# Row means over 536 MB: one single row at each end, zones of 94, 18 and 16 rows, and a last row shared with ScalarE

## The chip, the cores and the metric

The kernel runs on one core of one Trainium2 chip. The metric is device time in microseconds (us): the median of several executions. The time before is 1243.16 us, the median of three runs (1243.15 to 1243.31).

## The reference

The input is 64 x 256 x 8192 numbers in float32, and the output is the mean over the last axis:

```
def setup_inputs():
    return {
        "x": np.random.randn(64, 256, 8192).astype(np.float32),
    }

def reference(x: np.ndarray) -> np.ndarray:
    return np.mean(x, axis=2)
```

That is 16384 rows of 8192 numbers (32 KB a row), each summed and multiplied by 1/8192. 536.87 MB are read and 64 KB written.

## The kernel before, in words

The 16384 rows are spread over 128 partitions, so every partition owns 128 rows (OWN). They aren't dealt out as one block. ZONE = [95, 17, 16] (L27) cuts the rows of memory in three zones: in the first zone each partition owns 95 neighbouring rows, in the second 17, in the third 16. Inside a zone the rows of one partition lie one behind the other in memory, and the next partition begins 95, 17 or 16 rows further on: the row stride of the zone. Each zone has a store of its own at the end.

The work is a stream of pairs. A pair is two rows for each of the 128 partitions, 64 KB a partition and 8 MB in all. Three buffers (buf0 to buf2) of 64 KB a partition hold one pair each. The order of everything is written out by hand for each engine, with semaphores between them:

- SyncE (SP) issues all DMAs on one queue. It first issues the pair for buf0, which is a mixed one: the upper half is the first row of zone 1, in two pieces of 1 MB and 3 MB (L108, L109), and the lower half is the last row of zone 0 (L112). Two pairs for buf1 and buf2 follow (L114). Then a loop of 15 rounds (ROUNDS, L118) waits until a buffer is free and loads the next pair of zone 0 into it (L121), and 15 loads written out one by one do the rest (L127). The last two rows come in five pieces (L133, the bounds in cuts, L43); the fifth goes to a small tensor of its own, fin. SP then waits for GpSimd, stores zones 0 and 1 (L136), waits for the very last sum and stores zone 2 (L140).
- VectorE (DVE) reduces one pair with one tensor_reduce (L168, in a loop of 20 rounds of three; L178 for two of the last three). Pair 62, the last whole one, and the last two rows are summed by the helper halves (L149, L151): it adds the first half of a piece to its second half, element by element, and accumulates the sum over the columns in the same instruction. A piece of n columns so costs an instruction of n/2 columns.
- ScalarE (ACT) sums a share of four of the five last pieces (mine, L44) with an activation that copies and accumulates (L207). Its partial sums and those of VectorE are written behind the fifth piece in fin, so that the last halves (L199) sums the fifth piece and all partial sums at once and scales them.
- GpSimd (POOL) multiplies the sums by 1/8192 (L97) in four operations, after all rows but the last are summed.

A buffer's way round is: SP loads it (in_sems), VectorE reduces it (free_sems), SP loads it again. The change touches the sizes (L27 to L46), the order of loads in SP, the tail of VectorE and ScalarE, and GpSimd's operations.

Of the kernel before, what the change touches and what calls it, by code (L numbers as in the profile page):

```python
# [6 lines left out]
ADD = mybir.AluOpType.add  # L7
X = mybir.AxisListType.X
COPY = mybir.ActivationFunctionType.Copy


def bass_global_avg_pool_1d_kernel(
# [4 lines left out]
    P = 128  # L17
    ALIGN = 4096
    B, C, L = x.shape
    rows = B * C  # L20
    inv = 1.0 / float(L)

    OWN = rows // P
    ZONE = [95, 17, 16]  # L27
    FROM = [0, ZONE[0], ZONE[0] + ZONE[1]]
    EARLY, LATE = FROM[2], ZONE[2]
    NB = OWN // 2 - 1  # L30
    NBUF = 3
    PAIRS0 = ZONE[0] // 2
    ROUNDS = PAIRS0 // NBUF
    assert rows % P == 0 and sum(ZONE) == OWN and NB % NBUF == 0
    assert ZONE[0] % 2 == 1 and ZONE[1] % 2 == 1
    assert (PAIRS0 + 1) % NBUF == 0 and NB - PAIRS0 - 1 > NBUF
    LOADS0 = (NB - PAIRS0 - 1) // NBUF
    first_row = lambda g: 2 * g - 2 if g <= PAIRS0 else 2 * g
    FIRST = L // 4


    U = L // 256
    cuts = [0, L + 29 * U, L + 169 * U, L + 217 * U, L + 240 * U, 2 * L]  # L43
    mine = [29 * U, 50 * U, 17 * U, 8 * U]  # L44
    LAST = cuts[5] - cuts[4]
    NPART = 8  # L46

    flat = x.rearrange("b c l -> (b c) l")
    out_flat = out.rearrange("b c -> (b c)")
    zone = [  # L50
        flat[P * f : P * (f + n), :].rearrange("(p r) l -> p (r l)", p=P)
        for f, n in zip(FROM, ZONE)
    ]
# [2 lines left out]
        for f, n in zip(FROM, ZONE)  # L56
    ]

    with ExitStack() as ctx:
        sb = lambda n, s: ctx.enter_context(nc.sbuf_tensor(n, s, F32))  # L60
        sem = lambda n: ctx.enter_context(nc.semaphore(n))
        res = sb("res", [P, OWN - 1])
        scaled = sb("scaled", [P, EARLY])
        ends = sb("ends", [P, LATE])
        fin = sb("fin", [P, LAST + NPART])
        sb("pad", [P, (-nc.sbuf_base % ALIGN) // 4])
        bufs = [sb(f"buf{i}", [P, 2 * L]) for i in range(NBUF)]

        in_sems = [sem(f"in_sem{i}") for i in range(NBUF)]
        free_sems = [sem(f"free_sem{i}") for i in range(NBUF)]  # L70
        first_sem = sem("first_sem")
        mixed_sem = sem("mixed_sem")
        chunk_sems = [sem(f"chunk_sem{c}") for c in range(5)]
        owned_sem = sem("owned_sem")
        part_d = sem("part_d")
        part_a = sem("part_a")
        pool_sem = sem("pool_sem")
        late_sem = sem("late_sem")
        out_sem = sem("out_sem")
        end_sem = sem("end_sem")  # L80

        tail = bufs[0]
        part = lambda n: fin[:, LAST + n : LAST + n + 1]

        eng = nc.gpsimd
        eng.memset(part(NPART - 1), 0.0).then_inc(part_d, 1)  # L88
        eng.wait_ge(free_sems[0], LOADS0 + 1)
        eng.wait_ge(owned_sem, 4)  # L90
        for dst, src in [
            (scaled[:, 0 : ZONE[0] - 1], res[:, 2 : ZONE[0] + 1]),
            (scaled[:, ZONE[0] - 1 : ZONE[0] + 1], res[:, 0:2]),
            (scaled[:, ZONE[0] + 1 : EARLY], res[:, ZONE[0] + 1 : EARLY]),
            (ends[:, 0 : LATE - 1], res[:, EARLY : OWN - 1]),
        ]:
            eng.tensor_scalar(dst, src, inv, None, op0=mybir.AluOpType.mult).then_inc(  # L97
                pool_sem, 1
            )


        eng = nc.sync
        def rows_of(n, k):
            z = 2 if n >= FROM[2] else 1 if n >= FROM[1] else 0
            return zone[z][:, (n - FROM[z]) * L : (n - FROM[z] + k) * L]

        a, z = rows_of(ZONE[0] - 1, 1), rows_of(ZONE[0], 1)
        eng.dma_start(bufs[0][:, L : L + FIRST], z[:, 0:FIRST]).then_inc(first_sem, 16)  # L108
        eng.dma_start(bufs[0][:, L + FIRST : 2 * L], z[:, FIRST:L]).then_inc(  # L109
            mixed_sem, 16  # L110
        )
        eng.dma_start(bufs[0][:, 0:L], a).then_inc(in_sems[0], 16)  # L112
        for g in range(1, NBUF):
            eng.dma_start(bufs[g][:], rows_of(first_row(g), 2)).then_inc(in_sems[g], 16)  # L114
        src = rows_of(first_row(NBUF), ROUNDS * NBUF * 2).rearrange(
            "p (i b w) -> b p i w", i=ROUNDS, b=NBUF
        )
        with eng.Fori(0, ROUNDS) as i:  # L118
            for b in range(NBUF):
                eng.wait_ge(free_sems[b], 1).then_inc(free_sems[b], -1)  # L120
                eng.dma_start(bufs[b][:], src[b][:, bass.ds(i, 1), :]).then_inc(  # L121
                    in_sems[b], 16
                )
        for g in range(PAIRS0 + 1, NB):
            b = g % NBUF
            eng.wait_ge(free_sems[b], (g - PAIRS0 - 1) // NBUF + 1)
            eng.dma_start(bufs[b][:], rows_of(first_row(g), 2)).then_inc(in_sems[b], 16)  # L127
        eng.wait_ge(free_sems[0], LOADS0 + 1)
        two = rows_of(2 * NB, 2)
        for c in range(5):  # L130
            a, z = cuts[c], cuts[c + 1]
            dst = tail[:, a:z] if c < 4 else fin[:, 0:LAST]
            eng.dma_start(dst, two[:, a:z]).then_inc(chunk_sems[c], 16)  # L133
        eng.wait_ge(pool_sem, 4)
        for z in range(2):
            eng.dma_start(  # L136
                out_zone[z], scaled[:, FROM[z] : FROM[z] + ZONE[z]]
            ).then_inc(out_sem, 16)
        eng.wait_ge(late_sem, 1)
        eng.dma_start(out_zone[2], ends[:]).then_inc(end_sem, 16)  # L140
        eng.wait_ge(out_sem, 32)
        eng.wait_ge(end_sem, 16)

        eng = nc.vector

        def halves(ap, to, done, scale=1.0):  # L149
            n = ap.shape[1] // 2  # L150
            eng.tensor_tensor_reduce(  # L151
                ap[:, 0:n],
                ap[:, 0:n],
                ap[:, n : 2 * n],
                scale=scale,
                scalar=0.0,
                op0=ADD,
                op1=ADD,
                accum_out=to,
            ).then_inc(done, 1)  # L160

        eng.wait_ge(first_sem, 16)
        eng.wait_ge(mixed_sem, 16)
        sums = res[:, 0 : 2 * (NB - NBUF)].rearrange("p (i b j) -> p i b j", b=NBUF, j=2)
        with eng.Fori(0, NB // NBUF - 1) as i:
            for b in range(NBUF):
                eng.wait_ge(in_sems[b], 16).then_inc(in_sems[b], -16)  # L167
                eng.tensor_reduce(  # L168
                    sums[:, bass.ds(i, 1), b, :],
                    bufs[b][:].rearrange("p (j l) -> p j l", j=2),  # L170
                    X,
                    ADD,
                ).then_inc(free_sems[b], 1)
        for b in range(NBUF):
            g = NB - NBUF + b
            eng.wait_ge(in_sems[b], 16)
            if b < 2:
                eng.tensor_reduce(  # L178
                    res[:, 2 * g : 2 * g + 2],
                    bufs[b][:].rearrange("p (j l) -> p j l", j=2),  # L180
                    X,
                    ADD,
                ).then_inc(free_sems[0] if b == 0 else owned_sem, 1)
            else:
                for j in range(2):
                    halves(
                        bufs[b][:, j * L : (j + 1) * L],
                        res[:, 2 * g + j : 2 * g + j + 1],
                        owned_sem,
                    )  # L190
        eng.wait_ge(chunk_sems[0], 16)
        halves(tail[:, 0:L], res[:, 2 * NB : 2 * NB + 1], owned_sem)
        for c in range(1, 4):
            eng.wait_ge(chunk_sems[c], 16)
            halves(tail[:, cuts[c] + mine[c] : cuts[c + 1]], part(3 + c), part_d)
        eng.wait_ge(chunk_sems[4], 16)
        eng.wait_ge(part_a, 4)
        eng.wait_ge(part_d, 4)
        halves(fin, ends[:, LATE - 1 : LATE], late_sem, inv)  # L199


        eng = nc.scalar
        for c in range(4):
            eng.wait_ge(chunk_sems[c], 16)
            a = cuts[c] if c else L
            ap = tail[:, a : a + mine[c]]
            eng.activation(ap, ap, COPY, accum_out=part(c)).then_inc(part_a, 1)  # L207


# [26 lines left out]
```

## Time and profile before

| what | value |
|---|---|
| median of the runs | 1243.16 us (1243.15 to 1243.31) |
| the profiled execution | 1243.06 us |
| its span, first to last instruction | 1241.7 us |
| VectorE busy | 1084.1 us, 76 instructions |
| ScalarE busy | 5.2 us |
| GpSimd busy | 2.9 us |
| moved by DMA | 536.94 MB, 432 GB/s over the span |

The profile is that of one execution, and its 1243.06 us is 1.36 us longer than its span: that is time before the first and after the last instruction. "Idle before" in a row is the time that the engine waited just ahead of the instructions in it, with what ended the wait. The chain is followed back from the last instruction. Windows give the busy time of each engine between two points of the span, with the DMA engines' busy share and their rate at the end of the line. The timeline's first column is the start in us from the start of the span, and the second is the duration. A row of a DMA issue ends with the time from issue to landing.

### The profile page before, as it was taken

What the parts mean: (1) busy time and instruction counts of PE and PEld (TensorE: products, weight loads), DVE (VectorE), ACT (ScalarE), POOL (GpSimd) and SP (SyncE); (2) the same over time, 40 slices, a digit from 0 to 9 for tenths busy, and PEclk for the clock granted to TensorE, in tenths of its full rate; (3) what the DMA queues carried; (4) which work ended last, traced back from release to release, by engine and by line L of the source; (5) the groups of instructions that cost most, each with busy time, mean ns of one, the idle gap of its engine ahead of it and who ended that gap; (6) DMA issues with size and microseconds to landing.
All of it is one profiled execution on the core that took longest, in us unless ns stands there. A gap on an engine that the chain in (4) does not pass through costs nothing. (4 is left out here: it accounts for less than half of the span.)

```text
span 1241.7 us, 549 instructions
## 1 busy us (share of the span) xinstructions
DVE 1084.1 (87%) x76; ACT 5.2 (0%) x9; POOL 2.9 (0%) x9
## 2 busy tenths in 40 slices
DVE  2898988989889898898898988989889898898987
ACT  0000000000000000000000000000000000000001
POOL 0000000000000000000000000000000000000000
DMA  9999999999999999999999999999999999999998
GB/s 405 439 439 439 439 435 410 439 439 439 439 439 433 412 439 439 439 439 439 426 418 439 439 439 439 439 422 422 439 439 439 439 439 422 422 439 439 439 439 374
DMA packets 10512, 536.94 MB, mean 432 GB/s; under 512 B 1552, under 2 KB 1552, under 8 KB 1936
## 3 DMA queue, kind: packets, MB, share of 16 engines
q1 hardware_dynamic: 10512, 536.94, 99.9%
HBM read 536.87 MB, written 0.07 MB: 432 GB/s over the span
## 5 line engine op out<-in xcount | busy, mean ns | idle before, releaser
L168 DVE TENSOR_REDUCE res<-buf 128x16384 f32 x60 | 1033.2, 17220 | 146.5 <-DVEq L167 146.5
L178 DVE TENSOR_REDUCE res<-buf 128x2 f32<-128x16384 f32 x2 | 34.4, 17220 | 4.0 <-DMA buf<-in_x_dram 4.0
L151 DVE CUSTOM_DVE_ANT_0 buf<-buf 128x4096 f32<-128x4096 f32 (+3 forms) x6 | 16.0, 2672 | 5.4 <-DMA buf<-in_x_dram 5.4
L207 ACT ACTIVATE buf<-buf 128x928 f32<-128x928 f32 (+3 forms) x4 | 3.6, 897 | 1233.7 <-DMA buf<-in_x_dram 1233.7
L97 POOL TENSOR_SCALAR scaled<-res 128x94 f32<-128x94 f32 (+2 forms) x3 | 2.4, 784 | 1235.0 <-DVE res L151 1234.8
L207 ACT ACT_TABLE_LOAD x1 | 1.3, 1283 | 0.7 <-PEq L221 0.7
L207 ACT ACTIVATION_READ_ACCUMULATOR buf<-buf 128x1 f32 x4 | 0.7, 187 | 0.0
L151 DVE CUSTOM_DVE_ANT_0 fin<-fin 128x260 f32<-128x260 f32 x1 | 0.4, 429 | 0.3 <-DMA fin<-in_x_dram 0.3
L97 POOL TENSOR_SCALAR ends<-res 128x15 f32<-128x15 f32 x1 | 0.3, 264 | 0.1
L151 DVE DVE_READ_ACCUMULATOR2_ANT res<- 128x1 f32 x3 | 0.3, 84 | 0.0
L151 DVE DVE_READ_ACCUMULATOR2_ANT fin<- 128x1 f32 x3 | 0.2, 81 | 0.0
L221 POOL MEMSET const-bfloat16-1.0<- 128x1 bf16 x1 | 0.1, 102 | 0.0
L221 POOL MEMSET const-uint8-127<- 128x1 uint8 x1 | 0.1, 102 | 0.0
L88 POOL MEMSET fin<- 128x1 f32 x1 | 0.1, 99 | 0.3 <-POOLq L221 0.3
L221 POOL MEMSET const-float32-0.0<- 128x1 f32 x1 | 0.1, 99 | 0.2 <-issue 0.2
L221 POOL MEMSET const-float32-1.0<- 128x1 f32 x1 | 0.1, 99 | 0.0
L151 DVE DVE_READ_ACCUMULATOR2_ANT ends<- 128x1 f32 x1 | 0.1, 82 | 0.0
## 6 DMA issues: line engine op xcount, KB each, us to landing
buf<-in_x_dram SPq DMA_DIRECT2D x1, 4560.0 KB, 32.2
buf<-in_x_dram SPq DMA_DIRECT2D x1, 4096.0 KB, 20.6
buf<-in_x_dram SPq DMA_DIRECT2D x1, 3072.0 KB, 11.4
buf<-in_x_dram SPq DMA_DIRECT2D x1, 2240.0 KB, 37.1
buf<-in_x_dram SPq DMA_DIRECT2D x1, 1024.0 KB, 4.6
buf<-in_x_dram SPq DMA_DIRECT2D x62, 40.3
buf<-in_x_dram SPq DMA_DIRECT2D x1, 768.0 KB, 38.5
buf<-in_x_dram SPq DMA_DIRECT2D x1, 368.0 KB, 39.0
```

The costliest lines, as they stand in the source:

```text
L88: eng.memset(part(NPART - 1), 0.0).then_inc(part_d, 1)
L97: eng.tensor_scalar(dst, src, inv, None, op0=mybir.AluOpType.mult).then_inc(pool_sem, 1)
L151: eng.tensor_tensor_reduce(ap[:, 0:n], ap[:, 0:n], ap[:, n : 2 * n], scale=scale, scalar=0.0, op0=ADD, op1=ADD, accum_out=to,).then_inc(do ...
L168: eng.tensor_reduce(sums[:, bass.ds(i, 1), b, :], bufs[b][:].rearrange("p (j l) -> p j l", j=2), X, ADD,).then_inc(free_sems[b], 1)
L178: eng.tensor_reduce(res[:, 2 * g : 2 * g + 2], bufs[b][:].rearrange("p (j l) -> p j l", j=2), X, ADD,).then_inc(free_sems[0] if b == 0 els ...
L207: eng.activation(ap, ap, COPY, accum_out=part(c)).then_inc(part_a, 1)
L221: nc = _bacc.Bacc("TRN2", target_bir_lowering=False, num_devices=1)
```

## The change

- The stream begins with one single row (the first of zone 2), in two pieces of 1 MB and 3 MB, in the lower half of buf2. VectorE sums it with halves, and a new semaphore, first_done, tells SP that buf2 may be loaded with pair 2.
- 63 pairs follow, all of rows of one zone. The zones are 94, 18 and 16 rows, so that zones 0 and 1 hold whole pairs, and zone 2 holds its first row, seven pairs and its last row. The loop in SP has 14 rounds instead of 15, and 18 loads instead of 15 are written out.
- The last pair (pair 62, in buf2) has a semaphore of its own, pair_sem. VectorE sums its first row and the first quarter of its second row; ScalarE sums the other three quarters (6144 columns) into side.
- One single row comes last, in four pieces of 4992, 1920, 768 and 512 columns, where two rows came in five pieces of 9120, 4480, 1536, 736 and 512 columns. ScalarE takes 1856, 640 and 224 columns of the first three.
- GpSimd scales rows 0 to 111 in one operation as soon as buf0 has been reduced for pair 57, and SP issues the stores of zones 0 and 1 right behind the last four loads. GpSimd later adds the two parts of the shared row (tensor_tensor), waits for that, and scales the 14 inner columns of zone 2. VectorE scales the first and the last row of zone 2 itself.

The diff, cut to its core:

```diff
-    ZONE = [95, 17, 16]
+    ZONE = [94, 18, 16]
...
-    ROUNDS = PAIRS0 // NBUF
+    ROUNDS = PAIRS0 // NBUF - 1
+    SINGLE = NBUF * (ROUNDS + 1)
...
-    cuts = [0, L + 29 * U, L + 169 * U, L + 217 * U, L + 240 * U, 2 * L]
-    mine = [29 * U, 50 * U, 17 * U, 8 * U]
+    cuts = [0, 156 * U, 216 * U, 240 * U, L]
+    mine = [58 * U, 20 * U, 7 * U]
...
+    def pair(g, k=1):
+        z = 0 if 2 * g < FROM[1] else 1 if 2 * g < FROM[2] else 2
+        a = 2 * g - FROM[z] + (z == 2)
+        return zone[z][:, a * L : (a + 2 * k) * L]
...
         eng = nc.gpsimd
-        eng.memset(part(NPART - 1), 0.0).then_inc(part_d, 1)
-        eng.wait_ge(free_sems[0], LOADS0 + 1)
-        eng.wait_ge(owned_sem, 4)
-        for dst, src in [
-            (scaled[:, 0 : ZONE[0] - 1], res[:, 2 : ZONE[0] + 1]),
-            (scaled[:, ZONE[0] - 1 : ZONE[0] + 1], res[:, 0:2]),
-            (scaled[:, ZONE[0] + 1 : EARLY], res[:, ZONE[0] + 1 : EARLY]),
-            (ends[:, 0 : LATE - 1], res[:, EARLY : OWN - 1]),
-        ]:
-            eng.tensor_scalar(dst, src, inv, None, op0=mybir.AluOpType.mult).then_inc(
-                pool_sem, 1
-            )
+        eng.wait_ge(free_sems[0], turn(NB) - 1)
+        eng.tensor_scalar(
+            scaled[:], res[:, 0:EARLY], inv, None, op0=mybir.AluOpType.mult
+        ).then_inc(pool_sem, 1)
+        eng.wait_ge(free_sems[0], turn(NB))
+        eng.wait_ge(owned_sem, 3)
+        eng.wait_ge(side_a, 1)
+        eng.tensor_tensor(
+            res[:, 2 * NB - 1 : 2 * NB], side[:, 0:1], side[:, 1:2], op=ADD
+        ).then_inc(joined_sem, 1)
+        eng.wait_ge(joined_sem, 1)
+        eng.tensor_scalar(
+            ends[:, 1 : LATE - 1], res[:, EARLY : 2 * NB], inv, None,
+            op0=mybir.AluOpType.mult,
+        ).then_inc(pool_sem, 1)
...
         eng = nc.sync
+        eng.dma_start(single[:, 0:FIRST], zone[2][:, 0:FIRST]).then_inc(first_sem, 16)
+        eng.dma_start(single[:, FIRST:L], zone[2][:, FIRST:L]).then_inc(mixed_sem, 16)
+        for g in range(NBUF):
+            if g == NBUF - 1:
+                eng.wait_ge(first_done, 1)
+            eng.dma_start(bufs[g][:], pair(g)).then_inc(in_sems[g], 16)
...
-        for g in range(PAIRS0 + 1, NB):
+        for g in range(SINGLE, NB):
             b = g % NBUF
-            eng.wait_ge(free_sems[b], (g - PAIRS0 - 1) // NBUF + 1)
-            eng.dma_start(bufs[b][:], rows_of(first_row(g), 2)).then_inc(in_sems[b], 16)
-        eng.wait_ge(free_sems[0], LOADS0 + 1)
-        two = rows_of(2 * NB, 2)
-        for c in range(5):
+            eng.wait_ge(free_sems[b], turn(g))
+            eng.dma_start(bufs[b][:], pair(g)).then_inc(
+                in_sems[b] if g < NB - 1 else pair_sem, 16
+            )
+        eng.wait_ge(free_sems[0], turn(NB))
+        row = zone[2][:, (LATE - 1) * L : LATE * L]
+        for c in range(4):
...
-        eng.wait_ge(pool_sem, 4)
+        eng.wait_ge(pool_sem, 1)
         for z in range(2):
             eng.dma_start(
                 out_zone[z], scaled[:, FROM[z] : FROM[z] + ZONE[z]]
             ).then_inc(out_sem, 16)
+        eng.wait_ge(pool_sem, 2)
         eng.wait_ge(late_sem, 1)
...
         eng = nc.vector
...
         eng.wait_ge(mixed_sem, 16)
+        halves(single, ends[:, 0:1], first_done, inv)
...
+        eng.wait_ge(pair_sem, 16)
+        halves(both[:, 0:L], res[:, 2 * NB - 2 : 2 * NB - 1], owned_sem)
+        halves(both[:, L : L + SIDE], side[:, 0:1], owned_sem)
+        for c in range(3):
             eng.wait_ge(chunk_sems[c], 16)
-            halves(tail[:, cuts[c] + mine[c] : cuts[c + 1]], part(3 + c), part_d)
-        eng.wait_ge(chunk_sems[4], 16)
-        eng.wait_ge(part_a, 4)
-        eng.wait_ge(part_d, 4)
+            halves(tail[:, cuts[c] + mine[c] : cuts[c + 1]], part(c), part_d)
+        eng.wait_ge(chunk_sems[3], 16)
+        eng.wait_ge(part_a, 3)
+        eng.wait_ge(part_d, 3)
         halves(fin, ends[:, LATE - 1 : LATE], late_sem, inv)
...
         eng = nc.scalar
+        eng.wait_ge(pair_sem, 16)
+        ap = both[:, L + SIDE : 2 * L]
+        eng.activation(ap, ap, COPY, accum_out=side[:, 1:2]).then_inc(side_a, 1)
+        for c in range(3):
             eng.wait_ge(chunk_sems[c], 16)
-            a = cuts[c] if c else L
-            ap = tail[:, a : a + mine[c]]
-            eng.activation(ap, ap, COPY, accum_out=part(c)).then_inc(part_a, 1)
+            ap = tail[:, cuts[c] : cuts[c] + mine[c]]
+            eng.activation(ap, ap, COPY, accum_out=part(3 + c)).then_inc(part_a, 1)
```

Here U is 32 columns, L is 8192, NB is 63, LATE is 16, EARLY is 112 and SIDE is 2048. turn(g) is the count that free_sems must have reached for the load of pair g.

More of the change, by code (lines that the diff above doesn't have):

```diff
@@ L32, in bass_global_avg_pool_1d_kernel @@
     PAIRS0 = ZONE[0] // 2
-    ROUNDS = PAIRS0 // NBUF
+    ROUNDS = PAIRS0 // NBUF - 1
+    SINGLE = NBUF * (ROUNDS + 1)
     assert rows % P == 0 and sum(ZONE) == OWN and NB % NBUF == 0
[L35 to L38, printed above, removed]
+    assert all(z % 2 == 0 for z in ZONE) and 2 * (NB - NBUF) >= EARLY
+    turn = lambda g: (g - SINGLE) // NBUF + 1
     FIRST = L // 4
     U = L // 256
-    cuts = [0, L + 29 * U, L + 169 * U, L + 217 * U, L + 240 * U, 2 * L]
-    mine = [29 * U, 50 * U, 17 * U, 8 * U]
-    LAST = cuts[5] - cuts[4]
-    NPART = 8
+    cuts = [0, 156 * U, 216 * U, 240 * U, L]
+    mine = [58 * U, 20 * U, 7 * U]
+    LAST = cuts[4] - cuts[3]
+    NPART = 6
+    SIDE = L // 4
     flat = x.rearrange("b c l -> (b c) l")
@@ L72, in bass_global_avg_pool_1d_kernel @@
         mixed_sem = sem("mixed_sem")
-        chunk_sems = [sem(f"chunk_sem{c}") for c in range(5)]
+        first_done = sem("first_done")
+        pair_sem = sem("pair_sem")
+        chunk_sems = [sem(f"chunk_sem{c}") for c in range(4)]
         owned_sem = sem("owned_sem")
@@ L102, in bass_global_avg_pool_1d_kernel @@
-        eng = nc.sync
[L103 to L112, printed above, removed]
@@ L113, in bass_global_avg_pool_1d_kernel @@
-        for g in range(1, NBUF):
-            eng.dma_start(bufs[g][:], rows_of(first_row(g), 2)).then_inc(in_sems[g], 16)
-        src = rows_of(first_row(NBUF), ROUNDS * NBUF * 2).rearrange(
+        eng.wait_ge(free_sems[0], turn(NB) - 1)
[8 more added lines that the diff above has]
+        ).then_inc(joined_sem, 1)
@@ L116, in bass_global_avg_pool_1d_kernel @@
+        src = pair(NBUF, ROUNDS * NBUF).rearrange(
             "p (i b w) -> b p i w", i=ROUNDS, b=NBUF
@@ L173, in bass_global_avg_pool_1d_kernel @@
                 ).then_inc(free_sems[b], 1)
-        for b in range(NBUF):
-            g = NB - NBUF + b
+        for g in range(NB - NBUF, NB - 1):
+            b = g % NBUF
             eng.wait_ge(in_sems[b], 16)
[L177 to L190, printed above, removed]
@@ L191, in bass_global_avg_pool_1d_kernel @@
-        eng.wait_ge(chunk_sems[0], 16)
-        halves(tail[:, 0:L], res[:, 2 * NB : 2 * NB + 1], owned_sem)
-        for c in range(1, 4):
+            eng.tensor_reduce(
+                res[:, 2 * g : 2 * g + 2],
+                bufs[b][:].rearrange("p (j l) -> p j l", j=2),
+                X,
+                ADD,
+            ).then_inc(free_sems[0] if b == 0 else owned_sem, 1)
+        eng.wait_ge(pair_sem, 16)
+        halves(both[:, 0:L], res[:, 2 * NB - 2 : 2 * NB - 1], owned_sem)
+        halves(both[:, L : L + SIDE], side[:, 0:1], owned_sem)
@@ L202, in bass_global_avg_pool_1d_kernel @@
         eng = nc.scalar
-        for c in range(4):
+        eng.wait_ge(pair_sem, 16)
+        ap = both[:, L + SIDE : 2 * L]
+        eng.activation(ap, ap, COPY, accum_out=side[:, 1:2]).then_inc(side_a, 1)
+        for c in range(3):
             eng.wait_ge(chunk_sems[c], 16)
-            a = cuts[c] if c else L
-            ap = tail[:, a : a + mine[c]]
-            eng.activation(ap, ap, COPY, accum_out=part(c)).then_inc(part_a, 1)
+            ap = tail[:, cuts[c] : cuts[c] + mine[c]]
+            eng.activation(ap, ap, COPY, accum_out=part(3 + c)).then_inc(part_a, 1)
```

11 lines of the change are left out of this document (8 added, 3 removed).

## The prediction

> **What bounds the kernel now.** I read the page first: busy shares and slices, then the chain that ended last, then the transfers.
>
> ```profile
> DVE 1084.1 (87%) x76; ACT 5.2 (0%) x9; POOL 2.9 (0%) x9
> ...
> DMA  9999999999999999999999999999999999999998
> GB/s 405 439 439 439 439 435 410 439 439 439 439 439 433 412 439 439 439 439 439 426 418 439 439 439 439 439 422 422 439 439 439 439 439 422 422 439 439 439 439 374
> DMA packets 10512, 536.94 MB, mean 432 GB/s; under 512 B 1552, under 2 KB 1552, under 8 KB 1936
> ...
> DMA buf<-in_x_dram 3%; DMA fin<-in_x_dram 3%; DVE res L168 1%; DVE res L178 1%; SPq L133 0%; DVE fin L151 0%; DVEq L168 0%; DVE ends L151 0%
> ```
>
> The DMA engines are full in every slice but the last, and VectorE has 13% to spare. The dips in GB/s look like five hiccups. They are counting: at 434 GB/s one of 16 engines needs 65536 B x 16 / 434 GB/s = 2.42 us for a 64 KB packet, so a slice of 31.04 us holds 13 packet ends (439 GB/s) or 12 (405). If the stream really hiccuped, reductions would start late somewhere. The windows by zone, between starts of reductions, show that they don't:
>
> ```profile
> 22.49:930.65 908.16, 809.34 (x47) 0.00 (x0) 0.00 (x0) 1.00 1.00 434
> 930.65:1104.51 173.86, 154.98 (x9) 0.00 (x0) 0.00 (x0) 1.00 1.00 434
> 1104.51:1220.27 115.76, 103.32 (x7) 0.00 (x0) 0.00 (x0) 1.00 0.99 431
> ```
>
> First window: pairs 0 to 46, zone of 95 rows, 908.16 / 47 = 19.323 us a pair. Second: about the zone of 17, 173.86 / 9 = 19.318. Third: the zone of 16, six intervals (its seventh start is its end), 19.293. The timeline explains the odd one:
>
> ```profile
> 22.49 17.22 DVE L168 TENSOR_REDUCE res<-buf 128x16384 f32 x1 [22.49 <-DVEq L167]
> ...
> 39.99 19.66 SPq L121 DMA_DIRECT2D buf<-in_x_dram  x2
> ```
>
> ```profile
> 1162.48 17.22 DVE L168 TENSOR_REDUCE res<-buf 128x16384 f32 x1 [2.07 <-DVEq L167]
> ...
> 1181.58 17.22 DVE L178 TENSOR_REDUCE res<-buf 128x2 f32<-128x16384 f32 x1 [1.89 <-DMA buf<-in_x_dram]
> ...
> 1200.96 17.22 DVE L178 TENSOR_REDUCE res<-buf 128x2 f32<-128x16384 f32 x1 [2.16 <-DMA buf<-in_x_dram]
> 1220.27 4.42 DVE L151 CUSTOM_DVE_ANT_0 buf<-buf 128x4096 f32<-128x4096 f32 x1 [2.09 <-DMA buf<-in_x_dram]
> ```
>
> The step from the loop (1162.48) to the first reduction outside it (1181.58) is 19.10 us, the next one 19.38: inside the loop a reduction starts some 0.2 us later after its data. Corrected by 0.2, the third window is (115.76 + 0.2) / 6 = 19.327. So three row strides, 95, 17 and 16 rows, run within 0.01 us of 19.323 us a pair: the rate of the stream doesn't depend on the zone. A reduction takes 17.22, so 2.1 us are spare in every pair.
>
> The start is read from issue and landing:
>
> ```profile
> 0.73 0.39 SPq L108 DMA_DIRECT2D buf<-in_x_dram  x1
> 1.17 0.43 SPq L109 DMA_DIRECT2D buf<-in_x_dram  x1
> 1.65 0.42 SPq L112 DMA_DIRECT2D buf<-in_x_dram  x1
> ```
>
> ```profile
> buf<-in_x_dram SPq DMA_DIRECT2D x1, 4096.0 KB, 20.6
> buf<-in_x_dram SPq DMA_DIRECT2D x1, 3072.0 KB, 11.4
> ...
> out_dram<-scaled SPq DMA_DIRECT2D x1, 47.5 KB, 1.6
> out_dram<-scaled SPq DMA_DIRECT2D x1, 8.5 KB, 1.6
> out_dram<-ends SPq DMA_DIRECT2D x1, 8.0 KB, 1.4
> ```
>
> The first row is complete at 1.17 + 11.4 = 12.57, the first pair at 1.65 + 20.6 = 22.25. And the end, from the chain and the timeline:
>
> ```profile
> 1200.62 39.18 DMA fin<-in_x_dram
> ...
> 1239.83 0.43 DVE fin L151
> ```
>
> ```profile
> 1231.01 4.43 DVE L151 CUSTOM_DVE_ANT_0 buf<-buf 128x4096 f32<-128x4096 f32 x1 [1.97 <-DMA buf<-in_x_dram]
> ...
> 1236.35 1.66 DVE L151 CUSTOM_DVE_ANT_0 buf<-buf 128x1440 f32<-128x1440 f32 x1 [0.91 <-DMA buf<-in_x_dram]
> ...
> 1238.24 0.69 DVE L151 CUSTOM_DVE_ANT_0 buf<-buf 128x496 f32<-128x496 f32 x1 [0.22 <-DMA buf<-in_x_dram]
> ...
> 1239.14 0.41 DVE L151 CUSTOM_DVE_ANT_0 buf<-buf 128x240 f32<-128x240 f32 x1 [0.20 <-DMA buf<-in_x_dram]
> ...
> 1240.29 0.33 SPq L140 DMA_DIRECT2D out_dram<-ends  x1
> ```
>
> The last piece lands at T = 1200.62 + 39.18 = 1239.80, VectorE starts on it 0.03 later, the last store goes at 1240.29 and lands 1.4 later, at the span's end. All pieces were waited for: VectorE was idle before each. The time is start + stream + 1.9 us, and only T or those 1.9 us can move it.
>
> **The change part by part.**
>
> *Order and zones.* The same 536.87 MB is read. One row comes first as 1 MB and 3 MB, as now, then 63 pairs, then one row in four pieces. Zones of 94 and 18 rows replace 95 and 17. No row shows these strides; the nearest, above, lie within 0.005 us of 19.323 (the third, corrected one within 0.01). I take no change; bounds from those rows, 0.005 x 63 = 0.3 us either way.
>
> *Number of transfers.* 70 loads become 69. What a small one costs shows in the tail: from the last pair's landing, about 1220.25, to T are 19.55 us for five pieces, against 19.32 for one pair in one transfer: 0.23 us for four extra pieces, about 0.06 each. Now three extra pieces: 0.17.
>
> So the new T, step by step: first row at 12.57; 63 pairs x 19.323 = 1217.35, so the last pair at 1229.92; the last row 19.323 / 2 = 9.66 and 0.17 for its cuts: **T = 1239.75**, 0.05 earlier.
>
> *New wait on SP (first_done).* Pair 2 goes into the upper buffer, where the single row was, and waits for VectorE: 12.57 + 4.43 = 17.0 us. Behind it in SP stand the loop's loads, the first of them waiting for a reduction that can't start before pair 0 lands at 12.57 + 19.32 = 31.9. Pairs 0 and 1 are queued until 51.2, so the queue doesn't run dry; the cover is 34 us. In the loop a load is issued as its buffer is freed: now at 39.99, when 1.7 us of the current pair and all of the next are queued. The same lead of one pair stays. Cost nothing.
>
> *The first row's own addition* on VectorE lies in the wait for pair 0, free. In the loop nothing changes.
>
> *The tail on VectorE and ScalarE.* Counted back from T, with the cuts' bytes at 19.323 us per 64 KB and 0.06 a cut, the pieces land at T - 0.66 (as now: 1239.80 - 1239.14), T - 1.62, T - 3.95, and the last pair at T - 9.84. VectorE's prices lie on a line of about 1.03 ns a column (0.41, 0.69, 1.66, 4.43 above), ScalarE's on 0.83:
>
> ```profile
> L207 ACT ACTIVATE buf<-buf 128x1600 f32<-128x1600 f32 x1 | 1.5, 1537 | 4.3 <-DMA buf<-in_x_dram 4.3
> ...
> L207 ACT ACTIVATE buf<-buf 128x928 f32<-128x928 f32 x1 | 1.0, 977 | 1229.0 <-DMA buf<-in_x_dram 1229.0
> L207 ACT ACTIVATION_READ_ACCUMULATOR buf<-buf 128x1 f32 x4 | 0.7, 187 | 0.0
> ```
>
> (1537 - 977) / 672 = 0.83 ns. VectorE: the pair's first row 4.43, a quarter of the second (1024 columns) 0.69 + 528 x 1.03 = 1.23; ready at T - 4.2, before T - 3.95. Then 1568 columns 1.79, ready at T - 2.1 before T - 1.62; 640 columns 0.84, ready at T - 0.75 before T - 0.66; 272 columns 0.45, ready at T - 0.2. ScalarE: 6144 columns 1.54 + 4544 x 0.00083 = 5.32 and 0.19, ready at T - 4.3; 1856 columns 1.75 + 0.19, ready at T - 2.0; 640 columns 0.74 + 0.19, ready at T - 0.7; 224 columns 0.39 + 0.19, ready at T - 0.1. Every piece is done before the next lands, though with 0.1 us to spare at the end. If one is late by that, its lateness goes into the end, some 0.1 us. Cost nothing. Since the end waits for T now and then, sharing the second row can't gain; it only keeps up.
>
> *GpSimd and the stores.* Scaling rows 0 to 111 becomes one operation after pair 57, far ahead of the end. The two large stores are then issued right behind the four last loads, at about T - 29, and stand in the queue behind them; now they go at 1238.50, also before T, and land 1.6 us later. The last store keeps its place: 0.49 us behind T. I take nothing. Bounds: 0.1 us gained if the stores now in front of the last one hinder it; if they are carried out before the last load, they cost what 256 small packets take. Nearest row: 128 packets of 2 KB of the last piece in 0.66 us, so at most 1.3 us.
>
> *GpSimd's two late operations.* At T - 4 it adds the two sums of the shared row, then scales 14 columns. How they fare beside VectorE is shown by
>
> ```profile
> L97 POOL TENSOR_SCALAR scaled<-res 128x16 f32<-128x16 f32 x1 | 1.7, 1672 | 0.1
> ...
> L97 POOL TENSOR_SCALAR ends<-res 128x15 f32<-128x15 f32 x1 | 0.3, 264 | 0.1
> ```
>
> The same operation took 264 ns for 15 columns and 1672 ns for 16: the long one lay beside VectorE's 1.66 us at 1236.35. [...]
>
> Worked from the rows: behind VectorE's addition of 1568 columns the first ends at about T - 2, the second, if it misses that gap, behind 640 or 272 columns by T - 0.2; the store waits for VectorE until T + 0.49 anyway. [...] I take nothing; bounds 0 to 0.5.
>
> **The sum.** T 0.05 us earlier, the 1.9 us behind it the same: the span 1241.65 instead of 1241.7. The profiled execution took 1243.06, 1.36 outside the span, so 1243.01; the runs' median stands 0.10 above it, which gives 1243.1 (rounded).
>
> **The rivals.**
> 1. *The stream slows with the new strides* (slower). Place: the 63 pairs' reads. Against it: three strides at one rate. For it: 94 and 18 rows are not among them. Price: if every pair took the longest interval seen between two reductions outside the loop, 19.38, it is 0.057 x 63 = 3.6 us: **1246.7**. It decides from 19.363 us a pair on, 0.04 more (2.5 us in 63). Chance 0.06.
> 2. *The stream quickens* (faster), were 95 the odd one out: by the third window uncorrected, 19.293, it is 0.030 x 63 = 1.9 us, **1241.2**; beyond 0.2% it needs 19.283. Against it: 17 and 16 rows ran no faster. Chance 0.04 in all, taken as beyond 0.2%.
> 3. *The early stores get between the last loads*: up to 1.3 us, **1244.4**. Against it: one queue, and now the stores, issued before T, don't visibly delay the last piece. Chance 0.05.
> 4. *The late GpSimd operations hold up the end*: a second one that misses every gap ends behind VectorE's last addition, 0.5 us, **1243.6**. Against it: three gaps of 0.1 to 0.5 us. Chance 0.03.
> 5. *The change does what it says without effect*: my forecast. It evens out the tail, and the tail was already waiting for the DMA. **1243.1**, chance 0.82.
>
> **How the numbers follow.** 0.2% is 2.5 us, about what a measurement of this kernel can tell from no change. Cases 3, 4 and 5 lie within it: 0.90. Faster 0.04, slower 0.06. The range runs from 1243.1 less 0.3 (stream), 0.1 (stores) and 0.1 (the runs' own spread), 1242.6, to case 3's 1244.4; that leaves out cases 1 and 2, 0.10.
>
> **What would show it.** Right: pairs at 19.32 us in all zones; last piece landing at 1239.7 to 1239.8 with VectorE idle before each piece; a load for pair 2 at about 17 us with no later gap in the DMA row; ScalarE's long piece near 5.3 us. Wrong: pairs beyond 19.36 or below 19.28 us; the last addition waiting for ScalarE, GpSimd or VectorE instead of the DMA; the last piece taking over 0.7 us behind the one before it.

## The result, and the profile after

The changed kernel takes 1245.97 us (median of 13 runs, 1245.82 to 1246.22); beside it the kernel before took 1243.16 (13 runs, 1243.11 to 1243.32). The ratio is 1.0022, with a 95% interval of 1.0015 to 1.003. The forecast was 1243.1 within 1242.6 to 1244.4: the kernel became 2.8 us slower, and the range did not hold it.

The page of the changed kernel shows the same picture as before, a DMA that is full all along:

```profile
span 1244.6 us, 535 instructions
...
DVE 1081.2 (87%) x76; ACT 9.9 (1%) x9; POOL 2.7 (0%) x7
...
DMA  9999999999999999999999999999999999999998
GB/s 404 438 438 438 438 436 415 430 438 438 438 438 438 413 430 438 438 438 438 438 413 430 438 438 438 438 438 413 430 438 438 438 438 438 415 428 438 438 438 373
DMA packets 10368, 536.94 MB, mean 431 GB/s; under 512 B 1536, under 2 KB 1536, under 8 KB 1920
```

The full slices read 438 GB/s instead of 439. That one digit is the result: the stream is slower everywhere, at no particular place. The windows from the first to the last reduction of the loop give it exactly, first of the kernel before, then of the changed kernel:

```profile
22.49:1162.48 1139.99, 1015.98 (x60) 0.00 (x0) 0.00 (x0) 1.00 1.00 434
```

```profile
32.48:1174.69 1142.21, 1015.96 (x60) 0.00 (x0) 0.49 (x1) 1.00 1.00 433
```

The loop has 60 reductions, so either window holds 59 pairs: 1139.99 / 59 = 19.322 us a pair before, 1142.21 / 59 = 19.359 after, 0.037 more. For 63 pairs that is 2.4 us of the 2.9 between the spans (1241.7 and 1244.6). Some 0.3 come from the start (a difference between two traces more than between the kernels, as the point on the start below shows) and 0.2 from the tail. The timeline of the changed kernel:

```profile
13.03 4.43 DVE L153 CUSTOM_DVE_ANT_0 buf<-buf 128x4096 f32<-128x4096 f32 x1 [13.03 <-DMA buf<-in_x_dram]
...
32.48 17.22 DVE L171 TENSOR_REDUCE res<-buf 128x16384 f32 x1 [15.01 <-DVEq L170]
49.98 19.65 SPq L123 DMA_DIRECT2D buf<-in_x_dram  x2
51.84 17.22 DVE L171 TENSOR_REDUCE res<-buf 128x16384 f32 x1 [2.14 <-DVEq L170]
```

and its end:

```profile
1193.85 17.22 DVE L180 TENSOR_REDUCE res<-buf 128x2 f32<-128x16384 f32 x1 [1.94 <-DMA buf<-in_x_dram]
...
1232.57 5.32 ACT L200 ACTIVATE buf<-buf 128x6144 f32<-128x6144 f32 x1 [1230.57 <-DMA buf<-in_x_dram]
1232.58 4.42 DVE L153 CUSTOM_DVE_ANT_0 buf<-buf 128x4096 f32<-128x4096 f32 x1 [2.14 <-DMA buf<-in_x_dram]
...
1238.30 0.19 POOL L101 TENSOR_TENSOR res<-side 128x1 f32<-128x1 f32 x1 [84.53 <-DVE side L153]
...
1238.53 1.79 DVE L153 CUSTOM_DVE_ANT_0 buf<-buf 128x1568 f32<-128x1568 f32 x1 [0.38 <-DMA buf<-in_x_dram]
1238.58 1.86 POOL L105 TENSOR_SCALAR ends<-res 128x14 f32<-128x14 f32 x1
...
1240.91 0.82 DVE L153 CUSTOM_DVE_ANT_0 buf<-buf 128x640 f32<-128x640 f32 x1 [0.58 <-DMA buf<-in_x_dram]
...
1241.88 0.44 DVE L153 CUSTOM_DVE_ANT_0 buf<-buf 128x272 f32<-128x272 f32 x1
...
1242.59 0.43 DVE L153 CUSTOM_DVE_ANT_0 fin<-fin 128x259 f32<-128x259 f32 x1 [0.26 <-DMA fin<-in_x_dram]
```

VectorE is still idle ahead of every piece of the last row, a reduction takes 17.22 us as before, and no engine has become the bound. So the question is why every load is slower.

**What the diff doesn't show.** The diff ahead of the prediction leaves out the lines that allocate the small tensors: res and fin become smaller (fin has 6 columns for partial sums instead of 8), and side is new. In both kernels a filler, pad, is to bring buf0 to a multiple of 4096 bytes (ALIGN): its length is what is missing from the end of the tensors allocated so far. In the built program each of these tensors begins on a multiple of 32 bytes of its partition. Before, fin was 520 columns, 2080 bytes, and ended at byte 19616 of its partition, a multiple of 32; 216 columns of filler then end at 20480 = 5 x 4096. In the changed kernel fin has 518 columns, 2072 bytes, from 17568 to 19640. The filler of 210 columns is worked out from 19640, but begins at 19648 and ends at 20488, and buf0 begins at the next multiple of 32: **20512, 32 bytes behind 5 x 4096**. buf1 and buf2 follow at 65536 bytes each and are off by the same 32.

Theory: the 32 bytes slow every load into the buffers. Rival A: the strides of 94 and 18 rows, or the odd first row of zone 2. Rival B: the first row, read 16 rows apart, puts the stream in a slower step.

### The profile page after: what moved, and what is told of

Same layout as the page of the kernel before. It is cut to its first block, busy times and chain, and to the rows that moved or that the text cites. A ratio compares the mean times of both kernels' runs of the same rounds, so it can differ in the third digit from the quotient of the medians.

```text
span 1244.6 us, 535 instructions
## 1 busy us (share of the span) xinstructions
DVE 1081.2 (87%) x76; ACT 9.9 (1%) x9; POOL 2.7 (0%) x7
## 2 busy tenths in 40 slices
DMA packets 10368, 536.94 MB, mean 431 GB/s; under 512 B 1536, under 2 KB 1536, under 8 KB 1920
## 5 line engine op out<-in xcount | busy, mean ns | idle before, releaser
L153 DVE CUSTOM_DVE_ANT_0 buf<-buf 128x4096 f32<-128x4096 f32 (+4 forms) x6 | 13.1, 2188 | 16.3 <-DMA buf<-in_x_dram 16.1
L200 ACT ACTIVATE buf<-buf 128x6144 f32<-128x6144 f32 x1 | 5.3, 5323 | 1230.6 <-DMA buf<-in_x_dram 1230.6
L204 ACT ACTIVATE buf<-buf 128x1856 f32<-128x1856 f32 (+2 forms) x3 | 2.9, 959 | 1.2 <-DMA buf<-in_x_dram 1.1
## 6 DMA issues: line engine op xcount, KB each, us to landing
buf<-in_x_dram SPq DMA_DIRECT2D x1, 3072.0 KB, 11.7
out_dram<-scaled SPq DMA_DIRECT2D x1, 47.0 KB, 29.7
```

Source lines behind the costliest of these rows:

```text
L153: eng.tensor_tensor_reduce(ap[:, 0:n], ap[:, 0:n], ap[:, n : 2 * n], scale=scale, scalar=0.0, op0=ADD, op1=ADD, accum_out=to,).then_inc(do ...
L200: eng.activation(ap, ap, COPY, accum_out=side[:, 1:2]).then_inc(side_a, 1)
L204: eng.activation(ap, ap, COPY, accum_out=part(3 + c)).then_inc(part_a, 1)
```

## The experiments

Each was timed in five rounds beside the kernel before on the same chip: 11 runs a kernel, and 32 or 33 of the kernel before, whose median lay between 1243.21 and 1243.23. The intervals of single ratios are 0.001 wide to either side (about 1.2 us); differences of some tenths are read from the medians and from the traces, with the spread beside them.

### The filler alone, in both directions

The changed kernel with the filler mended:

```diff
-        sb("pad", [P, (-nc.sbuf_base % ALIGN) // 4])
+        sb("pad", [P, (-((nc.sbuf_base + 31) // 32 * 32) % ALIGN) // 4])
```

> The changed kernel with one line mended: the filler ahead of the buffers is made so long that buf0 begins at byte 20480 of each partition, a multiple of 4096, as in the kernel before; in the changed kernel it begins at 20512, 32 bytes behind. Theory (the 32 bytes slow every load): pairs at 19.32 us instead of 19.36, first row complete near 12.6 us instead of 12.9, 1243.1 us. Rival A (row strides of 94 and 18, or the odd first row of zone 2): pairs stay at 19.36, 1246.0 us. Rival B (the first row is read with a stride of 16 rows by 16 engines that start together, which sets a slower pattern for the whole stream): also 1246.0 us.

Measured: 1243.63 us (1243.35 to 1244.07), ratio 1.0003 [0.9994, 1.0012]. The time of the theory, 1243.1, was not quite reached (what is left is looked at below), and the first row was not complete earlier: it landed 11.7 us after its issue in both forms. The same 32 bytes put into the kernel before:

```diff
-        sb("pad", [P, (-nc.sbuf_base % ALIGN) // 4])
+        sb("pad", [P, (-nc.sbuf_base % ALIGN) // 4 + 8])
```

> The kernel before with 8 more columns of filler: buf0 begins at byte 20512 of each partition, nothing else differs. Theory (32 bytes off slow every load): pairs at 19.36 us, first row later by 0.3 to 0.4, 1245.8 us. Rivals A and B: 1243.2 us, since order and strides are those of before.

Measured: 1245.85 us (1245.66 to 1245.98), ratio 1.0021 [1.0012, 1.003]. Its window over the same 59 pairs:

```profile
22.86:1165.07 1142.21, 1015.98 (x59) 0.00 (x0) 0.00 (x0) 1.00 1.00 433
```

19.359 us a pair, that of the changed kernel to the last digit, with the zones, the order and the tail of the kernel before. The theory is shown from both sides: taking the 32 bytes away takes 2.3 us of the 2.8 away, and adding them alone costs 2.6. Rivals A and B, by which the first run had to stay at 1246.0 and the second at 1243.2, fall as the cause of the slow stream.

### Which boundary counts

The same line with 16, 32, 64, 128 and 512 columns in place of 8.

> The kernel before with buf0 at byte 20544, a multiple of 64 but not of 4096. Which boundary counts isn't known. If it is 64 bytes: 1243.2 us with pairs at 19.32. If it is a larger one (128 to 4096): 1245.8 us with pairs at 19.36. Rivals A and B: 1243.2 us.

> The kernel before with buf0 at byte 22528, a multiple of 2048 but not of 4096. If the boundary that counts is 4096: 1245.8 us; if it is 2048 or less: 1243.2 us. Rivals A and B: 1243.2 us.

> The kernel before with buf0 at byte 20992, a multiple of 512 but not of 1024. 2048 cost nothing, 64 cost 2.3 us. If the boundary that counts is 512 or less: 1243.2 us with pairs at 19.32. If it is 1024 or 2048: 1245.5 to 1245.9 us with pairs at 19.35 to 19.36.

> The kernel before with buf0 at byte 20608, a multiple of 128 but not of 256. If the boundary that counts is 128: 1243.2 us. If it is 256 or larger: 1245.0 to 1245.9 us, and if the cost falls with the distance from the boundary as from 32 to 64 bytes (2.6 to 2.3 us), about 1245.

> The kernel before with buf0 at byte 20736, a multiple of 256 but not of 512. 512 cost nothing, 128 cost 2.1 us. If the boundary that counts is 256: 1243.2 us. If it is 512: 1244.9 to 1245.3 us with pairs at 19.34 to 19.35.

| buf0 behind a multiple of 4096 by | median us | runs | ratio to before, 95% interval |
|---|---|---|---|
| 32 bytes | 1245.85 | 1245.66 to 1245.98 | 1.0021 [1.0012, 1.003] |
| 64 | 1245.49 | 1245.24 to 1245.61 | 1.0018 [1.0009, 1.0027] |
| 128 | 1245.35 | 1245.19 to 1245.55 | 1.0016 [1.0007, 1.0026] |
| 256 | 1243.21 | 1243.05 to 1243.4 | 1.0 [0.999, 1.0009] |
| 512 | 1243.22 | 1243.1 to 1243.34 | 1.0 [0.9991, 1.0009] |
| 2048 | 1243.2 | 1243.11 to 1243.49 | 1.0 [0.9991, 1.0009] |

Among these distances the boundary is 256 bytes, and the 4096 of ALIGN is more than is needed here. Of what was expected, a cost that falls evenly with the distance from the boundary did not come out: it is 2.6 us at 32 bytes, 2.3 at 64 and 2.1 at 128, and from 128 to 256 bytes it drops to nothing. Why it shrinks a little from 32 to 128 bytes no run shows. The edits move only the buffers that the loads write to, and a reduction of one still takes 17.22 us, so the cost lies with the loads' destination; which part of the chip sets the boundary was not shown.

### One, two or three buffers

Filler was placed between buffers, so that only some of them are 32 bytes off (the others on multiples of 256):

```diff
-        bufs = [sb(f"buf{i}", [P, 2 * L]) for i in range(NBUF)]
+        gaps = [0, 8, 0]
+        bufs = []
+        for i in range(NBUF):
+            if gaps[i]:
+                sb(f"gap{i}", [P, gaps[i]])
+            bufs.append(sb(f"buf{i}", [P, 2 * L]))
```

(here buf1 and buf2; [8, 56, 0] moves buf0 alone, [0, 8, 56] buf1 alone, [8, 0, 56] buf0 and buf1. The run with buf2 alone off has a filler of 8 columns ahead of buf2, written out.)

> The kernel before with 8 columns of filler between buf1 and buf2: buf0 and buf1 stay on multiples of 4096, buf2 begins 32 bytes behind one. If misplaced bytes cost each load into them by itself: every third pair is slow, a third of 2.6 us, 1244.0 to 1244.1 us, pairs at 19.33 to 19.34 us on average. If one misplaced load puts the stream in a slower step for good: 1245.8 us.

Measured: 1243.36 us (1243.16 to 1243.6), 0.13 more than before. Both answers that I had written down were wrong: it is neither a third of 2.6 nor all of it. Four more runs asked whether it is the buffer or the count.

> The kernel before with buf0 alone 32 bytes behind a multiple of 256 (buf1 and buf2 on multiples of 256). With buf2 alone off, the time was 1243.36, hardly more than before, where a cost for each load by itself would have given 1244.1. If buf0 (with the first pair and the last rows in it) is what counts: 1245 or more. If one misplaced load of three is made up for by the two others: 1243.2 to 1243.4.

> The kernel before with buf1 alone 32 bytes behind a multiple of 256. If buf1 is what counts: 1245 or more. If one misplaced load of three is made up for: 1243.2 to 1243.4.

> The kernel before with buf1 and buf2 32 bytes behind a multiple of 256 and buf0 on one. If one well placed load of three makes up for the two others: 1243.2 to 1243.4. If each load behind a misplaced one is what costs, a third of 2.6 us: 1244.1. If two of three cost two thirds: 1244.9.

> The kernel before with buf0 and buf1 32 bytes behind a multiple of 256 and buf2 on one. The same three answers as for buf1 and buf2: 1243.2 to 1243.4, 1244.1 or 1244.9; if the two runs differ, it is the buffer and not the count.

| buffers off by 32 bytes | median us | over before |
|---|---|---|
| buf0 | 1243.32 (1243.25 to 1243.4) | 0.11 |
| buf1 | 1243.26 (1243.21 to 1243.4) | 0.05 |
| buf2 | 1243.36 (1243.16 to 1243.6) | 0.13 |
| buf1 and buf2 | 1244.41 (1244.33 to 1244.5) | 1.20 |
| buf0 and buf1 | 1244.6 (1244.35 to 1245.16) | 1.39 |
| all three | 1245.85 (1245.66 to 1245.98) | 2.64 |

No buffer is special (of the three possible twos, buf0 with buf2 was not run); the count decides, and it doesn't add up evenly: the first of three is nearly free, each further one costs 1.1 to 1.4 us. The 95% intervals of the two twos, 1.001 [1.0001, 1.0019] and 1.0011 [1.0002, 1.002], lie above 1, those of the single buffers don't. The windows over the 59 pairs, buf2 alone and then buf1 with buf2, say the same:

```profile
22.68:1162.63 1139.95, 1015.98 (x59) 0.00 (x0) 0.00 (x0) 1.00 1.00 434
```

```profile
22.82:1163.85 1141.03, 1015.97 (x60) 0.00 (x0) 0.00 (x0) 1.00 1.00 434
```

19.321 and 19.339 us a pair, against 19.322 with none and 19.359 with all three. The single intervals say why. In the run with buf1 and buf2 off, four reductions in a row, from buf0, buf1, buf2 and again buf0, begin at:

```profile
893.07 17.22 DVE L173 TENSOR_REDUCE res<-buf 128x16384 f32 x1 [2.08 <-DVEq L172]
912.42 17.22 DVE L173 TENSOR_REDUCE res<-buf 128x16384 f32 x1 [2.14 <-DVEq L172]
931.78 17.22 DVE L173 TENSOR_REDUCE res<-buf 128x16384 f32 x1 [2.14 <-DVEq L172]
951.08 17.22 DVE L173 TENSOR_REDUCE res<-buf 128x16384 f32 x1 [2.07 <-DVEq L172]
```

The loads into buf1 and buf2 take 19.35 and 19.36 us, as with all three off, and the one into buf0 takes 19.30, less than the 19.32 with none off. Over the whole loop the mean step to a reduction, in us, by the buffer that it waits for, is:

| buffers off | buf0 | buf1 | buf2 |
|---|---|---|---|
| none | 19.321 | 19.324 | 19.320 |
| buf0 | 19.355 | 19.301 | 19.298 |
| buf1 | 19.310 | 19.341 | 19.309 |
| buf2 | 19.313 | 19.307 | 19.343 |
| buf1 and buf2 | 19.301 | 19.357 | 19.359 |
| buf0 and buf1 | 19.357 | 19.358 | 19.302 |
| all three | 19.362 | 19.359 | 19.358 |

So each misplaced load takes its longer time, 19.34 to 19.36 us, and the well placed loads between them make up for part or nearly all of it: they take 19.30 to 19.31, and 19.32 only among their like. That fits two limits in a row, of which the one that misplacing slows is a little the faster while the buffers are well placed. The making up is shown; the two limits are the author's reading of these numbers, no run shows them, and which part of the chip would hold which stays open.

### What is left when the buffers are in place

Mended, the changed kernel still took 0.42 us more than before by the medians, inside the interval of one comparison. The execution that was profiled is the slowest of the eleven (1244.07 us), and its windows show a slow passage at the start of the stream:

```profile
32.45:226.53 194.08, 172.20 (x10) 0.00 (x0) 0.00 (x0) 1.00 1.00 432
226.53:1173.11 946.58, 843.79 (x50) 0.00 (x0) 0.49 (x1) 1.00 1.00 434
```

The first ten pairs take 19.41 us each, the other 49 take 946.58 / 49 = 19.318. Here rivals A and B are asked again, for a smaller matter. First the first row's place:

```diff
-        eng.dma_start(single[:, 0:FIRST], zone[2][:, 0:FIRST]).then_inc(first_sem, 16)
-        eng.dma_start(single[:, FIRST:L], zone[2][:, FIRST:L]).then_inc(mixed_sem, 16)
+        odd = flat[P * 95 : P * 112, :].rearrange("(p r) l -> p (r l)", p=P)
+        eng.dma_start(single[:, 0:FIRST], odd[:, 0:FIRST]).then_inc(first_sem, 16)
+        eng.dma_start(single[:, FIRST:L], odd[:, FIRST:L]).then_inc(mixed_sem, 16)
```

> The changed kernel with its buffers aligned (as in the run before) and the single first row read from where the kernel before reads its first row, 17 rows apart instead of 16. It sums another row than the reference for 128 of the outputs. Aligned, the changed kernel still took 0.4 us more than the kernel before, and its profile showed some ten pairs of 19.36 to 19.55 us at the start of the stream. Theory B (a first row read 16 rows apart starts all DMA engines in a bad step with one another, and they take ten pairs to leave it): pairs at 19.32 from the start, 1243.1 to 1243.2 us. Theory A (the first pairs of the zone of 94 rows are slow when the engines are close together): unchanged, 1243.6 us.

Measured: 1243.47 us (1243.1 to 1243.75). Then zone 0's stride, and both edits at once:

```diff
+    zone[0] = flat[0 : P * 95, :].rearrange("(p r) l -> p (r l)", p=P)
     out_zone = [
```

> The changed kernel with its buffers aligned and the partitions of zone 0 set 95 rows apart instead of 94 (94 rows of each are read, so one row in 95 is left out and the next are other rows than the reference's); first row as in the changed kernel. Theory A (stride of 94 rows): the slow pairs at the start go, 1243.1 to 1243.2 us. Theory B (first row 16 rows apart): unchanged, 1243.6 us. If both this and the other change remove it, either is enough; if neither, the late load of pair 2 is what is left, 1243.6 us in both.

> The changed kernel with its buffers aligned, the first row read 17 rows apart and zone 0 with partitions 95 rows apart: both earlier edits at once (other rows than the reference's are summed in both places). Each alone left 0.25 to 0.3 us over the kernel before. If the strides are the rest: 1243.2 us. If the rest is the late load of pair 2, or the tail: 1243.4 to 1243.5 us.

Measured: 1243.50 us (1243.36 to 1243.61) for the stride alone, 1243.30 (1243.08 to 1243.39) with both. Over the kernel before: 0.42 with neither, 0.25 and 0.28 with one, 0.07 with both. Neither theory's number came out for a single edit; together they leave next to nothing. The traces, one execution each, lean to the first row: the first six intervals take 19.415 us a pair in the mended kernel, 19.322 with the first row moved, 19.358 with zone 0's stride alone and 19.332 with both (19.335 in the kernel before). The steps are of the size of the runs' own spread, so this points to the strides as a start-up cost of some 0.3 us and doesn't settle it.

Last, the new wait on SP by itself, in the kernel before:

```diff
         for g in range(1, NBUF):
+            if g == NBUF - 1:
+                eng.wait_ge(mixed_sem, 16)
             eng.dma_start(bufs[g][:], rows_of(first_row(g), 2)).then_inc(in_sems[g], 16)
```

> The kernel before in which SP issues the load of pair 2 only when its first row has landed, at about 12.6 us instead of 2.7: the new wait on SP by itself. Mine: the queue still holds two loads, 1243.2 us. If the shorter queue at the start is what is left of the difference: 1243.4 to 1243.5 us.

Measured: 1243.25 us (1243.11 to 1243.46), ratio 1.0001 [0.9991, 1.001]. A load of pair 2 issued ten microseconds later costs nothing that can be seen. In the changed kernel it is issued later still, at about 17.5 (VectorE's addition of the first row ends at 13.03 + 4.43); that wait was not run by itself.

No run is faster than the kernel before. The mended kernel ends at 1243.63, and with both strides of the kernel before, at 1243.30.

## Why the prediction was wrong, point by point

- **What bounds the kernel: right.** The stream sets the time before and after. The page of the changed kernel shows such dips again, while its pairs, averaged over six, stay between 19.358 and 19.362 us in the loop: that fits the counting of packets.
- **Order and zones: this is the step that failed.** It said that no change was to be taken, with 0.3 us either way, because three row strides run at one rate. Measured were 0.037 us a pair, 2.4 us in 63. The conclusion from the strides held in the main: with the buffers back in place the loop ran at 19.318 us a pair behind the first ten, even in the slowest execution, and some 0.4 us were left by the medians. But the bound left out the other end of every load. It priced where the bytes come from and not where they go: the diff changes res, fin and adds side, all ahead of the filler, and the filler's sum no longer comes out on a boundary. A check of where buf0 begins in the built program would have shown it; a price for it was in no row of the profile, and would have been a rival with a range of its own.
- **Rival 1 named the right symptom and its place**, all 63 pairs slower. It was to count from 19.363 us a pair on and forecast 1246.7; measured were 19.359, just short of that, and 1245.97. Its reason, the strides, was wrong, so that its symptom came true was luck, and it had a chance of 0.06.
- **Number of transfers: right in size.** With the buffers in place, the mended kernel needed 9.85 us from the last pair's landing to T, where 9.66 + 0.17 = 9.83 were forecast. Its rows: VectorE's start on the pair, taken as 0.02 us after it lands (what the chain of that run shows between a landing and the start behind it), and the last landing from the chain.

```profile
1230.90 4.43 DVE L153 CUSTOM_DVE_ANT_0 buf<-buf 128x4096 f32<-128x4096 f32 x1 [2.08 <-DMA buf<-in_x_dram]
```

```profile
1210.79 29.95 DMA fin<-in_x_dram
```

  That is 1240.73 (the sum 1210.79 + 29.95, rounded) less 1230.88. The 0.05 us of gain forecast for T is too small to be seen.
- **The new wait and the first row: right.** In the kernel before a wait until 12.6 us alone cost 0.02 us; in the changed one the loop's first load is issued at 49.98, with more than one pair queued ahead of it.
- **The tail: right.** ScalarE's 6144 columns took 5.32 us as worked out, VectorE's pieces 1.79, 0.82 and 0.44 against 1.79, 0.84 and 0.45; the spare time ahead of the pieces was 0.38, 0.58 and, from 1240.91 + 0.82 to 1241.88, 0.15 us. That sharing the row gained nothing is read from these waits, before and after; no run shares it alone.
- **GpSimd's late operations: right in their cost, half right in their course.** That either would stand behind an addition of VectorE was an estimate from one row of before (1672 ns beside an addition of 1.66 us). The first was to end behind VectorE's addition of 1568 columns, at about T - 2. It came through ahead of it, in 0.19 us at 1238.30, 4.3 us before T = 1242.57; the second began at 1238.58, 0.05 us behind VectorE's addition, and took 1.86 us for 14 columns instead of 0.26 for 15. It ended at 1240.44, 2.1 us before T, and cost nothing. The other way round, VectorE held up by GpSimd, does not show: the addition that the second one lay beside took 1.79 us, as forecast.
- **The stores: right.** Issued at about 1212.9 and 1213.4, they landed 29.7 and 29.6 us later, at 1242.6 and 1242.9, not ahead of the last piece:

```profile
out_dram<-scaled SPq DMA_DIRECT2D x1, 47.0 KB, 29.7
out_dram<-scaled SPq DMA_DIRECT2D x1, 9.0 KB, 29.6
out_dram<-ends SPq DMA_DIRECT2D x1, 8.0 KB, 1.4
```

```profile
1212.42 30.15 DMA fin<-in_x_dram
```

  The sum 1212.42 + 30.15 = 1242.57, from the chain's row for fin in the changed kernel, is the last piece's landing, 0.69 us behind the start on the one before it (1241.88); in the kernel before it was 0.66. Rival 3 did not happen, and the last store took 1.4 us again.
- **The start: not forecast.** The prediction took the first row's 12.57 us from the trace of before. In the changed kernel the row took 0.3 us more to land:

```profile
buf<-in_x_dram SPq DMA_DIRECT2D x1, 3072.0 KB, 11.7
```

  It was 11.4 before, issued at 1.17 in both. That is the profiled execution of before more than the change: in the profiles of all other runs, of either kernel, the first row's larger piece took 11.6 to 11.8 us. In the kernel before with buf0 512 bytes further on, at an unchanged median, the first reduction began at 22.85 instead of 22.49:

```profile
22.85 17.22 DVE L168 TENSOR_REDUCE res<-buf 128x16384 f32 x1 [22.85 <-DVEq L167]
```

## What to carry to other kernels

When a kernel is bound by a stream of large loads, look at where its buffers begin in memory after every change of any tensor allocated ahead of them: here a small one whose size was no multiple of 32 bytes cost 2.3 us through a filler that no longer came out even. Compute a filler from the place where it really begins, and state the boundary in the code as an assertion on the buffer's address, not as a formula. And bound a stream's rate at both of its ends: an argument from the source's strides says nothing about the destination.

## What the runs showed of the hardware that was not expected

- With its loads of 64 KB a partition beginning 128, 64 or 32 bytes behind a multiple of 256 bytes, the kernel took 0.17% to 0.21% longer (1245.35, 1245.49 and 1245.85 us against 1243.2), and no longer when they begin on one (1243.21, 1243.22 and 1243.2 us at 256, 512 and 2048 bytes).
- A misplaced load took 19.34 to 19.36 us with one, two or three buffers off, but the well placed ones made up for it: they took 19.32 us among their like and 19.30 to 19.31 beside a misplaced one. So with every third load misplaced the kernel lost 0.05 to 0.13 us, with two of three 1.2 to 1.4, with all of them 2.64.
- In two traces a start some hundredths earlier or later went with a sevenfold cost of a small GpSimd operation beside VectorE's additions; no run moved that start alone. In the kernel before, the scaling of 15 columns began at 1238.21, 0.03 us before an addition (1238.24), and took 0.26 us; in the changed kernel the scaling of 14 columns began 0.05 us behind an addition and took 1.86 us, VectorE's 1.79 and a little.

```profile
1238.21 0.26 POOL L97 TENSOR_SCALAR ends<-res 128x15 f32<-128x15 f32 x1
```
